# A hybrid attention and state-space layer: half of the opening's adaLN rows as TensorE products, the opening's orders written out, and attention loads one step ahead

## The chip, the cores and the metric

The kernel runs on one core of a Trainium2 chip. Its time is the device time of one execution in microseconds. Three runs of the kernel before were timed; the profile is of one more execution. The engines are TensorE (PE, with its weight loads as PEld), VectorE (DVE), ScalarE (ACT), GpSimd (POOL) and SyncE (SP), which issues nearly all DMA transfers. Each engine works through its own queue in order.

## The reference, cut to what matters

One layer over 2048 tokens of width 1024, in f32, and one conditioning vector `c`:

```python
mod = jax.nn.silu(c) @ w_ada[layer] + b_ada[layer]          # 1024 -> 6 * 1024
shift1, scale1, gate1, shift2, scale2, gate2 = jnp.split(mod, N_MOD, axis=-1)
h = modulate(rmsnorm(x, norm1_w[layer]), shift1, scale1)    # h * (1 + scale) + shift
x = x + gate1[:, None, :] * hybrid_mixer(h, ...)            # q, k, v, z, x/B/C, dt = h @ w_in
h = modulate(rmsnorm(x, norm2_w[layer]), shift2, scale2)    # attention and an SSD scan
x = x + gate2[:, None, :] * swiglu(h, w_gate_up[layer], w_down[layer])
return rmsnorm(x, final_norm_w)
```

`q` and `k` are turned by rotary tables (`rope`) whose angles come from `positions`. Nothing of the mixer can be computed before `shift1` and `scale1`, 2 x 1024 of the 6 x 1024 modulation values, are there.

## The kernel before, in words

The tokens are cut into four blocks of 512 (`b` 0 to 3). Activations stand with the feature on the partition, eight tiles of 128 x 512 per block. Each big product is made from operands split into a high and a low f32r half: `mm3` (L237 to L240) issues three matmuls, high by high, high by low, low by high. `weight` (L222) loads a weight tile into one of 5 `raw` buffers, ACT rounds it into the high half (L230), POOL subtracts for the low half (L231); six `w` buffers hold the pairs. `modulated` (L272) makes one tile of the normalized and modulated input: a DVE product (L274), the high half on ACT (L276), the low half on DVE (L277).

For each block the mixer's projections run one after the other: `queries`, `keys_values`, `convolved`, `gated`. They are Python generators, and PE's order is the order in which the generators are advanced (`manual_schedule` with PE among its engines means that PE issues in program order). `run(main, ratio)` advances a main generator; after each of its steps `tick` advances the side work (attention, the state-space scan, output projection) `ratio` steps, one step of `rest_of_ada`, and counts down the `pending` steps of the next block's norm. Engines that are not under `manual_schedule` get their order from the compiler, which simulates the program and lets a later instruction go ahead when its inputs and buffers are ready.

A modulation value is a dot product of silu(c) with a column of `w_ada`. The transposed matrix lies in memory as 48 rows of 128 x 1024; `ada` (L151) loads one row (512 KB, one DMA) and reduces it on DVE against `csil`, silu(c) copied to all partitions (L154). That gives 128 of the values, one column of `mod`. Columns 8 to 15 are `scale1`, 0 to 7 `shift1`. The other 32 rows are done later by `ada_later` (L156), in two halves of 256 KB with two `aw` buffers (L160, L165).

The opening is `first_norm` (L929) under `manual_schedule` for PE, DVE and SP. Eight tiles of x are loaded; ACT squares each (L940) and PE sums each square over the partitions with 4 products of two columns (L942). `root_of` takes the root on DVE, `spread` (L263) builds a diagonal and copies it over the partitions with one plain f32 product of 512 columns (L269). Then for each of the eight tiles the scale column is finished (L948), the tile modulated, and the reductions of a later pair of rows and the loads of q weights follow. After it `rope_tables` (L177) makes the sine and cosine tables: seven DVE steps each for sine and cosine and one ACT step each (L193), on three `s` buffers.

After the opening `queries(0, h)` (L342) makes q for the four token tiles of block 0 at once, 192 products of 256 columns into all four `d` banks of PSUM, and `rope` (L312) reads each bank with four DVE steps (L321, L322) before it is free. `keys_values` (L367) needs two `d` banks for each half of the block. The loads of x for the next block's norm are held behind the last load of x (`issue_after(last_load.ins)`, L1035).

`attentions` (L466) works through 4 tiles of 128 queries a block. Each starts with the loads of kv and q (L488, L489) and at once transposes both on PE (L493, L501); then come four steps of scores, with the tile before finished in between.

Of the kernel before, what the change touches and what calls it, by code (L numbers as in the profile page):

```python
# [17 lines left out]
P = 128  # L18
S = 2048
D = 1024  # L20
# [22 lines left out]
def hymba_layer(ctx, tc, xT, crow, pos, wada, vecs, rows, wq, wkv, wz, wx, wo, wgu, wd4, wd2, outT):  # L43
# [57 lines left out]
    vec = const([P, 116], "vec", pool=cst)  # L101
# [8 lines left out]
    conv_b, snw = vec[:, 104:112], vec[:, 112:116]  # L110
# [32 lines left out]
    def silu_c(i):  # L143
        cs, th = csil[:, i * T:(i + 1) * T], big("s", 3, pool=fw)
        nc.scalar.activation(th, cs, AF.Tanh, scale=0.5)
        nc.vector.scalar_tensor_tensor(cs, th, 1.0, cs, ALU.add, ALU.mult)
    mod = const([P, 48], "mod", pool=cst)
# [3 lines left out]
    def ada(i, m):  # L151
        w = m().rearrange("p h t -> p (h t)").bitcast(F32)
        nc.sync.dma_start(w, wada[i])
        nc.vector.tensor_tensor_reduce(w, w, csil, 0.5, b_ada[:, i:i + 1], ALU.mult, ALU.add, mod[:, i:i + 1])  # L154

# [21 lines left out]
    def rope_tables():  # L177
        posf = const([P, S // P], "posf", pool=ip)
        nc.vector.tensor_copy(posf, posi)
        ang = big("s", 3, pool=fw)  # L180
# [3 lines left out]
        for dst, turn in ((sin, 0.0), (cos, 0.25)):  # L184
            k, r = big("s", 3, pool=fw), big("s", 3, pool=fw)
# [6 lines left out]
            nc.vector.tensor_scalar(r, r, PI_IN, -PI_IN, ALU.min, ALU.max)  # L192
            nc.scalar.activation(dst.rearrange("p t j -> p (t j)"), r, AF.Sin)  # L193

# [27 lines left out]
    def weight(src, n, key, store):  # L222
# [8 lines left out]
        nc.gpsimd.tensor_tensor(lo, raw[:, :n], hi.bitcast(F32), ALU.subtract)  # L231
# [40 lines left out]
    def modulated(x, bc, scale, shift, into):  # L272
# [4 lines left out]
        nc.vector.scalar_tensor_tensor(lo, h, shift, hi.bitcast(F32), ALU.add, ALU.subtract)  # L277
# [64 lines left out]
    def queries(b, h):  # L342
        if b == 0:
            qb = [dense() for _ in range(NT)]
            for kp in range(KT // 2):
                ws = first_ws[kp] if kp < len(first_ws) else [weight(wq[c][kp], 512, (f"q{c}", kp), False)
                                                              for c in range(2)]
# [115 lines left out]
    def attentions(b, m):  # L463
# [20 lines left out]
        held = None  # L484
        for t in range(NT):
            gt = b * NT + t
            q, kv = m.m2(), m.m1()
            nc.sync.dma_start(kv, kv_d[gt])  # L488
            nc.sync.dma_start(q, q_d[gt])  # L489
# [19 lines left out]
            for j in range(4):  # L509
# [3 lines left out]
                if j == 3:  # L513
                    probabilities(st, sms, slots)
                yield
# [413 lines left out]
    def first_norm():  # L929
        st, h, x0, ws = side_bank(0), [], [], []  # L930
# [4 lines left out]
        for d in range(2):  # L935
            ada(8 + d, common.m4)
            ada(d, extra.m4)
        for d in range(KT):
            sq = tmp()
            nc.scalar.activation(sq, x0[d], AF.Square)  # L940
            for t in range(NT):
                nc.tensor.matmul(st[:, 2 * t:2 * t + 2], sq[:, t * P:(t + 1) * P], ones[:, 0:2],  # L942
                                 start=d == 0 and t == 0, stop=d == KT - 1 and t == NT - 1, skip_group_check=True)
        y = root_of(st, NT)
        bc = spread(y, bc=side_bank(1))
        ada(10, common.m4)
        for d in range(KT):
            nc.vector.scalar_tensor_tensor(scl1[:, d:d + 1], mod[:, 8 + d:9 + d], 1.0, n1w[:, d:d + 1],  # L948
                                           ALU.add, ALU.mult)
            h.append(modulated(x0[d], bc, scl1[:, d:d + 1], sh1[:, d:d + 1], operand()))  # L950
            if d + 2 < KT:
                ada(2 + d, extra.m4)
            if d + 3 < KT:
                ada(11 + d, common.m4)
            if d % 2 == 0 and d < 6:
# [225 lines left out]
```

## Time and profile before

| | us |
|---|---|
| runs timed, median (lowest, highest) | 2439.4 (2439.01, 2440.95) |
| the profiled execution | 2434.49 |
| its span, first to last instruction | 2432.8 |
| mean granted TensorE clock | 0.965 |
| PE / DVE / POOL / ACT busy | 2261.8 / 1461.9 / 1262.3 / 967.3 |
| first q product on PE | 32.42 |
| first product of keys_values on PE | 98.32 |

Times within the profile count from the start of the span. In the groups by line, the columns after the bar are busy time, mean ns of one, and the idle time of the engine just before, with what ended it. In a timeline the columns are start, duration, engine, line, operation, output and inputs; in brackets stands the idle time before it and what ended that. In the list of waits: us in total, how often, and the longest. In the table of windows each engine's busy time in that stretch stands with its number of instructions. PE's matmuls overlap, so their rate is read from one start to the next, not from the duration. A helper's instructions all have the helper's line: L238 to L240 are every split product.

### The profile page before, as it was taken

To read this page: it belongs to the slowest core of one execution; us is meant where nothing else is said; L and a number is where in the kernel's file an instruction comes from. 1 tells how busy PE (TensorE), PEld (TensorE's weight loads), DVE (VectorE), ACT (ScalarE), POOL (GpSimd) and SP (SyncE) were. 2 spreads that over 40 slices of the span, in tenths; PEclk is the share of its full clock that TensorE was granted. 3 is DMA by queue.
4 is the path that set the end of the run, shared out by engine and by line. 5 is a ranking of instruction groups with operands and counts; after the bars stand their busy time and mean duration, and the time that the engine had idled before them with its cause. 6 is when DMAs were issued, how large, how long until landed. Compare 5 with 4: busy or idle time off the path is not lost.

```text
span 2432.8 us, 33013 instructions
## 1 busy us (share of the span) xinstructions
PE 2261.8 (93%) x11254; PEld 1891.9 (78%) x11254; DVE 1461.9 (60%) x2519; ACT 967.3 (40%) x2004; POOL 1262.3 (52%) x1249
## 2 busy tenths in 40 slices
PE   6587999999999799999999999899899999999996
PEld 5567989887988588888887877677688888878785
DVE  7876874764445965578675434438855555554544
ACT  2354552655245545433334323224333333333332
POOL 3653743534122864679885234137766666643432
PEclk9798999999999799999999999999899999999998
DMA  7699866868874322233235555764322222263441
GB/s 274 210 331 316 294 228 204 279 218 275 287 241 159 96 78 83 81 111 100 88 95 167 197 177 158 249 206 136 130 87 84 86 79 78 78 228 98 145 157 53
DMA packets 244457, 403.82 MB, mean 166 GB/s; under 512 B 21952, under 2 KB 68032, under 8 KB 244288
## 3 DMA queue, kind: packets, MB, share of 16 engines
q1 hardware_dynamic: 243136, 400.66, 50.0%
q8 instruction: 89, 1.46, 0.2%
q10 hardware_dynamic: 1152, 1.05, 0.1%
q14 instruction: 80, 0.66, 0.1%
HBM read 307.19 MB, written 94.44 MB: 165 GB/s over the span
## 4 chain that ended last, share of the span: by engine, by line
PE 77%; DVE 8%; DMA 5%; issue 4%; POOL 3%; ACT 3%; SPq 1%; POOLq 0%; DVEq 0%; ACTq 0%
PE d L238 11%; PE d L240 11%; PE d L239 11%; PE d L803 8%; PE d L805 8%; PE d L804 8%; PE am L238 1%; PE am L239 1%; PE am L240 1%; POOL w L231 1%; PE at L574 1%; DMA t<-act 1%; DMA t<-in_xT_dram 1%; PE sm L683 1%; PE st L803 1%
## 5 line engine op out<-in xcount | busy, mean ns | idle before, releaser
L752 ACT ACTIVATE w<-raw 128x512 fp32r<-128x512 f32 x308 | 193.5, 630 | 531.7 <-PE d L240 251.0
L803 PE MATMUL d<-b,w 128*128 128x512 f32 x924 | 372.7, 405 | 17.4 <-ACT b L783 9.6
L804 PE MATMUL d<-b,w 128*128 128x512 f32 x924 | 370.8, 401 | 7.2 <-DVE b L779 5.1
L805 PE MATMUL d<-b,w 128*128 128x512 f32 x924 | 368.9, 399 | 0.0
L238 PE MATMUL d<-a,w 128*128 128x512 f32 (+1 forms) x720 | 281.1, 398 | 12.4 <-ACT a L871 11.5
L239 PE MATMUL d<-a,w 128*128 128x512 f32 (+1 forms) x720 | 281.5, 391 | 1.7 <-DVE a L747 1.7
L240 PE MATMUL d<-a,w 128*128 128x512 f32 (+1 forms) x720 | 282.3, 392 | 0.0
L753 POOL TENSOR_TENSOR w<-raw,w 128x512 fp32r<-128x512 f32 x88 | 120.1, 1365 | 304.8 <-ACT w L752 292.0
L753 POOL TENSOR_TENSOR w<-s,w 128x512 fp32r<-128x512 f32 x132 | 188.6, 1429 | 126.1 <-ACT w L752 117.6
L882 DVE SCALAR_TENSOR_TENSOR x<-d,mod,x 128x512 f32<-128x512 f32 (+1 forms) x182 | 130.9, 725 | 197.6 <-PE d L240 197.3
L238 PE MATMUL d<-w,hl 128*128 128x256 f32 (+1 forms) x640 | 194.8, 304 | 43.3 <-DVE s L322 19.9
L803 PEld LDWEIGHTS d<-b,w 128*128 128x128 f32 x924 | 175.9, 191 | 60.6 <-ACT b L783 13.3
L753 DVE TENSOR_TENSOR w<-raw,w 128x512 fp32r<-128x512 f32 x220 | 191.1, 869 | 43.3 <-ACT w L752 40.7
L804 PEld LDWEIGHTS d<-b,w 128*128 128x128 f32 x924 | 176.4, 191 | 46.7 <-DVE b L779 6.8
L805 PEld LDWEIGHTS d<-b,w 128*128 128x128 f32 x924 | 176.5, 191 | 39.9
L240 PE MATMUL d<-w,hl 128*128 128x256 f32 (+1 forms) x640 | 190.8, 298 | 4.6 <-DVE hl L277 4.6
L239 PE MATMUL d<-w,hl 128*128 128x256 f32 (+1 forms) x640 | 189.7, 296 | 0.0
L238 PEld LDWEIGHTS d<-a,w 128*128 128x128 f32 x720 | 137.1, 191 | 47.5 <-ACT a L871 15.5
L238 PEld LDWEIGHTS d<-w,hl 128*128 128x128 f32 x640 | 130.8, 204 | 48.4 <-issue 20.9
L239 PEld LDWEIGHTS d<-a,w 128*128 128x128 f32 x720 | 136.8, 190 | 34.4 <-DVE a L747 2.8
L248 POOL TENSOR_TENSOR t<-t 128x512 f32<-128x512 f32 (+1 forms) x84 | 106.7, 1271 | 108.5 <-ACT t L247 104.8
L240 PEld LDWEIGHTS d<-a,w 128*128 128x128 f32 x720 | 136.2, 189 | 30.3
(311 smaller groups left out, 5427.7 us busy)
## 6 DMA issues: line engine op xcount, KB each, us to landing
raw<-in_wgu_dram SPq DMA_DIRECT2D x176, 256.0 KB, 2.7
raw<-in_wd_dram SPq DMA_DIRECT2D x176, 256.0 KB, 2.7
w<-w_x SPq DMA_DIRECT2D x48, 512.0 KB, 4.9
w<-w_o SPq DMA_DIRECT2D x48, 512.0 KB, 4.6
act<-t SPq DMA_DIRECT2D x88, 256.0 KB, 2.1
t<-act SPq DMA_DIRECT2D x88, 256.0 KB, 4.7
t<-in_xT_dram SPq DMA_DIRECT2D x80, 256.0 KB, 4.3
aw<-in_wada_dram SPq DMA_DIRECT2D x64, 256.0 KB, 3.8
```

What stands on the lines that cost most here:

```text
L231: nc.gpsimd.tensor_tensor(lo, raw[:, :n], hi.bitcast(F32), ALU.subtract)
L238: nc.tensor.matmul(out, ahi, bhi, start=first, stop=False)
L239: nc.tensor.matmul(out, ahi, blo, start=False, stop=False)
L240: mm3.last = nc.tensor.matmul(out, alo, bhi, start=False, stop=last)
L248: eng.tensor_tensor(acc, acc, sq, ALU.add)
L574: nc.tensor.transpose(ps[:, (2 * s + r) * P:(2 * s + r + 1) * P], sm[:, r, s, :], ident)
L752: nc.scalar.activation(hi, x, AF.Copy)
L753: eng.tensor_tensor(lo, x, hi.bitcast(F32), ALU.subtract)
L803: nc.tensor.matmul(out, ahi, bhi, start=first and k == 0, stop=False, skip_group_check=True)
L804: nc.tensor.matmul(out, ahi, blo, start=False, stop=False, skip_group_check=True)
L805: mm3.last = nc.tensor.matmul(out, alo, bhi, start=False, stop=k == 3, skip_group_check=True)
L882: nc.vector.scalar_tensor_tensor(x, ps, gate2[:, c:c + 1], x, ALU.mult, ALU.add)
```

## The change

- The 16 rows of the first modulation: those of `mod` columns 8 to 13 and 0 to 5 that belong to tiles 2 to 5 stay reductions on DVE (`rows_of`, `reduced`: 8 rows). The other 8 rows (tiles 0, 1 and 6, 7) come as TensorE products: a new input `wadk` holds those columns of `w_ada` untransposed, in two batches of 4 loads of 512 KB. PE multiplies each 128 x 512 half load with one column of silu(c) (`ccol`) into one PSUM line, 8 products a batch; ACT copies the line out, PE turns it into columns by four small products, and three short DVE steps finish `mod` and `scl1`.
- The squares are summed over the eight tiles by DVE adds, so that PE sums over partitions with 4 calls.
- `opening` replaces `first_norm`, with ACT too in program order, and with the q products placed inside: PE's order is 4 sums, 6 products of the first batch, the spread, 2 products, the turning, q products of tiles 0 to 3, the second batch, its turning, q products of tiles 4 to 7.
- The low halves of block 0's q weights are made on DVE, not POOL.
- Half of the rotary tables is made at the very start, the other half after the last modulation; the tables and silu(c) use `m2` buffers, not `s`.
- q of block 0 takes two `d` banks and the side banks `sm` and `st`.
- What follows the opening, up to and with `keys_values(0)`, the start of `rest_of_ada` and the next block's norm, is under `issue_after(first_done.ins)`: its DVE instructions stand behind the last modulation. The norm of block 1 is begun after keys_values, with its later steps at ticks 11 and 15, not 17 and 21.
- `attentions` loads the first kv and q with two empty steps ahead of their use, and those of each later tile in the middle of the tile before.

```diff
+    def ada_loads(batch):
+        ws = [extra.m4().bitcast(F32) for _ in range(KT // 2)]
+        for w, src in zip(ws, wadk[batch]):
+            nc.sync.dma_start(w.rearrange("p h t -> p (h t)"), src)
+        return ws
+
+    def ada_products(ws, out, ks):
+        for k in ks:
+            nc.tensor.matmul(out[0:1, :], ccol[:, k:k + 1], ws[k // 2][:, k % 2, :], start=k == 0, stop=k == KT - 1)
+
+    def ada_columns(out, turned, d):
+        line = tmp()[0:1, :]
+        nc.scalar.copy(line, out[0:1, :])
+        for j in range(4):
+            nc.tensor.matmul(turned[:, 2 * j:2 * j + 2], line[:, j * P:(j + 1) * P], ones[0:1, 0:2], start=True, stop=True)
+        got = turned[:, 0:8].rearrange("p (j k) -> p j k", k=2)[:, :, 0]
+        for at, src in ((8 + d, got[:, 0:2]), (d, got[:, 2:4])):
+            nc.vector.scalar_tensor_tensor(mod[:, at:at + 2], src, 0.5, b_ada[:, at:at + 2], ALU.mult, ALU.add)
+        nc.vector.scalar_tensor_tensor(scl1[:, d:d + 2], mod[:, 8 + d:10 + d], 1.0, n1w[:, d:d + 2], ALU.add, ALU.mult)
...
-        nc.gpsimd.tensor_tensor(lo, raw[:, :n], hi.bitcast(F32), ALU.subtract)
+        (nc.vector if key[0][0] == "q" and not split_d else nc.gpsimd).tensor_tensor(lo, raw[:, :n], hi.bitcast(F32), ALU.subtract)
...
-            qb = [dense() for _ in range(NT)]
+            qb = [dense(), dense(), side_bank(2), side_bank(3)]
...
-        held = None
+        def load(t):
+            q, kv = m.m2(), m.m1()
+            nc.sync.dma_start(kv, kv_d[b * NT + t])
+            nc.sync.dma_start(q, q_d[b * NT + t])
+            return q, kv
+
+        held, nxt = None, load(0)
+        yield
+        yield
         for t in range(NT):
-            gt = b * NT + t
-            q, kv = m.m2(), m.m1()
-            nc.sync.dma_start(kv, kv_d[gt])
-            nc.sync.dma_start(q, q_d[gt])
+            gt, (q, kv) = b * NT + t, nxt
...
+                if j == 2 and t + 1 < NT:
+                    nxt = load(t + 1)
...
-    def first_norm():
...
+    def opening():
+        accs, h, x0 = tmp(), [], []
         for d in range(KT):
             x = extra.m2()
             x0.append(x)
-            last_load = nc.sync.dma_start(x, xT[0, d])
...
+            nc.sync.dma_start(x, xT[0, d])
+        tables = rope_tables()
+        silu_columns()
+        next(tables)
         for d in range(KT):
...
+            square_into(accs, x0[d], d == 0, nc.vector)
+        first = ada_loads(0)
...
+        for i in range(2):
+            silu_c(i)
+        st, line = side_bank(1), side_bank(0)
+        for t in range(NT):
+            nc.tensor.matmul(st[:, 2 * t:2 * t + 2], accs[:, t * P:(t + 1) * P], ones[:, 0:2], start=True, stop=True)
+        ada_products(first, line, range(0, 6))
         y = root_of(st, NT)
         bc = spread(y, bc=side_bank(1))
...
+        ada_products(first, line, range(6, 8))
+        ada_columns(line, side_bank(0), 0)
+        weights(0)
+        rows = [rows_of(2), rows_of(3)]
+        main = queries(0, h)
+        ready(0)
+        ready(1)
+        next(main)
+        weights(1)
+        reduced(2, rows[0])
+        ready(2)
+        rows.append(rows_of(4))
+        reduced(3, rows[1])
+        ready(3)
+        second = ada_loads(1)
+        next(main)
+        line = side_bank(0)
+        ada_products(second, line, range(8))
+        weights(2)
+        rows.append(rows_of(5))
+        reduced(4, rows[2])
+        ready(4)
+        reduced(5, rows[3])
+        ready(5)
+        ada_columns(line, side_bank(0), 6)
+        weights(3)
+        next(main)
+        ready(6)
+        ready(7)
+        next(main)
+        drain(tables)
+        return h, main
...
-        run(queries(0, h), 0)
-        with tc.issue_after(last_load.ins):
-            nxt = norm_ahead(1, (17, 21))
-        rest = rest_of_ada()
-        ada_rest.append(rest)
-        run(keys_values(0, h), 0)
+        with tc.issue_after(first_done.ins):
+            drain(main)
+            rest = rest_of_ada()
+            ada_rest.append(rest)
+            run(keys_values(0, h), 0)
+            nxt = norm_ahead(1, (11, 15))
```

Of the helpers inside `opening` that the cut leaves out, `weights(kp)` fetches and splits two q weight tiles, `rows_of(d)` loads the two rows of tile d into `common` `m4` buffers (there are four), `reduced(d, two)` reduces them and finishes `scl1`, and `ready(d)` is one `modulated`. `first_done` is the last DVE instruction of the last `modulated`.

More of the change, by code (lines that the diff above doesn't have):

```diff
@@ L143, in silu_c, with silu_columns @@
     def silu_c(i):
-        cs, th = csil[:, i * T:(i + 1) * T], big("s", 3, pool=fw)
+        cs, th = csil[:, i * T:(i + 1) * T], common.m2()
         nc.scalar.activation(th, cs, AF.Tanh, scale=0.5)
         nc.vector.scalar_tensor_tensor(cs, th, 1.0, cs, ALU.add, ALU.mult)
+    def silu_columns():
+        th = small([P, KT], "csc", 1, pool=ip)
+        nc.scalar.activation(th, ccol, AF.Tanh, scale=0.5)
+        nc.vector.scalar_tensor_tensor(ccol, th, 1.0, ccol, ALU.add, ALU.mult)
     mod = const([P, 48], "mod", pool=cst)
@@ L183, in rope_tables @@
                                 invf.unsqueeze(1).broadcast_to([P, S // P, HALF]), ALU.mult)
-        for dst, turn in ((sin, 0.0), (cos, 0.25)):
-            k, r = big("s", 3, pool=fw), big("s", 3, pool=fw)
+        turns = []
+        for turn in (0.0, 0.25):
+            k, r = common.m2(), common.m2()
             nc.vector.tensor_scalar(k, ang, 1.0 / (2 * math.pi), turn, ALU.mult, ALU.add)
@@ L276, in modulated @@
         nc.scalar.activation(hi, h, AF.Identity, bias=shift)
-        nc.vector.scalar_tensor_tensor(lo, h, shift, hi.bitcast(F32), ALU.add, ALU.subtract)
+        modulated.last = nc.vector.scalar_tensor_tensor(lo, h, shift, hi.bitcast(F32), ALU.add, ALU.subtract)
         return hi, lo
@@ L343, in queries @@
         if b == 0:
-            qb = [dense() for _ in range(NT)]
+            qb = [dense(), dense(), side_bank(2), side_bank(3)]
             for kp in range(KT // 2):
-                ws = first_ws[kp] if kp < len(first_ws) else [weight(wq[c][kp], 512, (f"q{c}", kp), False)
-                                                              for c in range(2)]
+                ws = first_ws[kp]
                 for e in range(2):
@@ new lines, in opening, with weights, rows_of, reduced @@
+        first = ada_loads(0)
+        def weights(kp):
+            first_ws.append([weight(wq[c][kp], 512, (f"q{c}", kp), False) for c in range(2)])
+        def rows_of(d):
+            m = common.m4().rearrange("p h t -> p (h t)").bitcast(F32)
+            n = common.m4().rearrange("p h t -> p (h t)").bitcast(F32)
+            nc.sync.dma_start(m, wada[8 + d])
+            nc.sync.dma_start(n, wada[d])
+            return m, n
+        def reduced(d, two):
+            for i, w in zip((8 + d, d), two):
+                nc.vector.tensor_tensor_reduce(w, w, csil, 0.5, b_ada[:, i:i + 1], ALU.mult, ALU.add, mod[:, i:i + 1])
+            nc.vector.scalar_tensor_tensor(scl1[:, d:d + 1], mod[:, 8 + d:9 + d], 1.0, n1w[:, d:d + 1],
+                                           ALU.add, ALU.mult)
@@ L947, in first_norm @@
[L947 to L955, printed above, removed]
-                ws.append([weight(wq[c][d // 2], 512, (f"q{c}", d // 2), False) for c in range(2)])
@@ L957, in first_norm @@
-        return h, last_load, ws
-    with tc.manual_schedule(engines={mybir.EngineType.PE, mybir.EngineType.DVE, mybir.EngineType.SP}):
-        for i in range(2):
-            silu_c(i)
-        h, last_load, first_ws = first_norm()
-        rope_tables()
+        ada_products(first, line, range(6, 8))
[7 more added lines that the diff above has]
+        weights(1)
@@ L965, in hymba_layer @@
+        ready(7)
+        next(main)
+        drain(tables)
+        return h, main
+    first_ws = []
+    with tc.manual_schedule(engines={mybir.EngineType.PE, mybir.EngineType.DVE, mybir.EngineType.SP,
+                                     mybir.EngineType.Activation}):
+        h, main = opening()
+        first_done = modulated.last
     nc.scalar.activation(neg_a, a_log, AF.Exp)
@@ L1131, in _layout @@
     out["wada"] = a(w_ada[0].T.reshape(48, P, D))
+    wk = w_ada[0].reshape(D, 6, 4, 2 * P)
+    out["wadk"] = a(np.stack([np.concatenate([wk[:, 1, i], wk[:, 0, i]], axis=1) for i in (0, 3)])
+                    .reshape(2, 4, 2, P, T).transpose(0, 1, 3, 2, 4).reshape(2, 4, P, 2 * T))
     cols = lambda v, n: v.reshape(n, P).T
```

26 lines of the change are left out of this document (11 added, 15 removed).

## The prediction

> **What bounds the kernel now.** I read the page's busy line and strip first, then the windows for the start, then who PE waited for, and last the timelines of the start.
>
> ```profile
> PE 2261.8 (93%) x11254; PEld 1891.9 (78%) x11254; DVE 1461.9 (60%) x2519; ACT 967.3 (40%) x2004; POOL 1262.3 (52%) x1249
> ...
> PE   6587999999999799999999999899899999999996
> ```
>
> PE carries the run: 9 tenths nearly everywhere. The exception is the left end, where the first two slices (61 us each) stand at 6 and 5. The windows there, whose columns are PE, PEld, DVE, ACT, POOL busy, granted clock, DMA share and GB/s:
>
> ```profile
> 0.00:32.40 32.40, 15.86 (x66) 14.23 (x66) 17.73 (x37) 9.36 (x16) 7.54 (x51) 1.00 0.89 343
> 32.40:78.70 46.30, 35.26 (x192) 32.17 (x192) 41.64 (x70) 12.02 (x20) 17.01 (x11) 0.82 0.60 189
> 78.70:98.30 19.60, 0.01 (x1) 0.01 (x1) 18.60 (x31) 6.61 (x10) 10.96 (x8) 0.60 0.62 202
> 98.30:112.40 14.10, 13.76 (x95) 13.49 (x96) 10.53 (x32) 4.75 (x9) 14.10 (x16) 0.83 0.57 186
> 100.00:240.00 140.00, 111.02 (x659) 99.39 (x659) 97.98 (x240) 68.66 (x157) 79.59 (x80) 0.90 0.91 315
> ```
>
> Up to 32.4 DMA works (0.89). From 32.4 to 98.3 DVE does: 60.2 us busy of 65.9, while PE does the 192 q products and then nothing for 19.6 us. Who PE waited for says why:
>
> ```profile
> PE d L238 <- DVE s L322: 19.9, 2, 19.6
> ...
> PE d L238 <- DVE so L411: 8.6, 2, 6.7
> ...
> PE am L493 <- DMA m<-kv: 8.4, 1, 8.4
> ...
> PE at L501 <- DMA m<-q: 2.3, 2, 1.4
> ```
>
> The first line is the gap. The q products fill all four `d` banks; rope must read one before keys_values has a bank; rope needs the tables, which DVE makes only after the last modulation, between rows of `ada_later`. The critical path of the opening is thus DVE: modulations, tables, rope, then PE.
>
> **The opening of the new kernel up to the first q product.**
>
> ```profile
> L940 ACT ACTIVATE t<-m x8: 612/629/630, 8.3 to 12.7; 128x512 f32<-128x512 f32 x8
> ```
> ```profile
> 9.09 13.79 PE L942 MATMUL am<-ones,t 128*128 128x2 f32 x64 [9.09 <-ACT t L940]
> ```
> ```profile
> L942 PEld LDWEIGHTS am<-ones,t x64: 288/333/338, 9.1 to 22.5; 128*128 128x128 f32 x64
> ```
> ```profile
> 754.48 1.02 PE L269 MATMUL sm<-t,ones 128*128 128x512 f32 x2
> 755.34 1.02 PE L269 MATMUL st<-t,ones 128*128 128x512 f32 x2
> ...
> 1638.11 2.05 PE L269 MATMUL am<-t,ones 128*128 128x512 f32 x2
> ```
> ```profile
> 76.65 0.69 DVE L182 TENSOR_TENSOR s<-posf,invf 128x512 f32<-128x512 f32 x1
> ```
> ```profile
> 124.40 0.57 ACT L393 COPY cin<-d 128x512 f32<-128x512 f32 x1
> ```
> ```profile
> 32.42 0.58 PE L238 MATMUL d<-w,hl 128*128 128x256 f32 x1 [2.08 <-ACT hl L276]
> ```
>
> The squares end at 13.3 as before (12.7 plus 0.63); their adding up, now on DVE, trails by one add of 0.69: 14.0. The first half of the tables lies ahead of that, while x still lands, and is covered. The 32 column sums of L942 (13.79 us, 0.43 a call) become four: 15.7.
>
> Next come eight products of a one-column weight with 512 columns of plain f32, with the spread after the sixth. None is in this trace; the nearest is the spread, L269, also plain f32 by 512: 0.86 us from one call to the next in the first two rows, and in the third one call with its tail takes 2.05, twice one row's 1.02, so I put a call there at 1.7. Nine calls cost 7.7 or 15.3. I take the higher price: L942's weight loads, at the same place and of the same type, took 333 ns (median, none under 288) from beginning to end. So 31.0, with 23.4 kept for the range. The root of the mean lies beside the first six.
>
> Then ACT copies the line (0.57), four small products turn it (0.43 each), and three short DVE steps, 0.5 as an estimate from the 0.69 of a wide one, give the modulation: 33.8. ACT is now in program order, so the casts of the first q weights and the first `hi` queue behind that copy. Two `lo` of weights now on DVE (1.4), one product and its `hi` (1.4) bring the first q product to 36.6. It was 32.42: this part loses 4.2.
>
> **From there to the end of the q products.**
>
> ```profile
> 41.12 1.28 DVE L154 CUSTOM_DVE_ANT_0 m<-m,csil,vec 128x1024 f32<-128x1024 f32 x1
> ...
> 47.50 2.31 DVE L154 CUSTOM_DVE_ANT_0 m<-m,csil,vec 128x1024 f32<-128x1024 f32 x1
> ...
> 50.98 0.75 DVE L274 SCALAR_TENSOR_TENSOR t<-m,scl,at 128x512 f32<-128x512 f32 x1
> 52.52 0.75 DVE L277 SCALAR_TENSOR_TENSOR hl<-t,mod,hl 128x512 fp32r<-128x512 f32 x1 [0.79 <-ACT hl L276]
> 53.19 1.28 DVE L154 CUSTOM_DVE_ANT_0 m<-m,csil,vec 128x1024 f32<-128x1024 f32 x1
> ...
> 73.95 1.82 DVE L277 SCALAR_TENSOR_TENSOR hl<-t,mod,hl 128x512 fp32r<-128x512 f32 x1
> ```
> ```profile
> 62.00 0.28 PE L240 MATMUL d<-w,hl 128*128 128x256 f32 x1
> 62.12 0.28 PE L238 MATMUL d<-w,hl 128*128 128x256 f32 x1
> ```
>
> DVE's list is written out by hand: the first `lo` 0.75; `ready(1)`, 2.2 as from 50.98 to 53.19, the wait for ACT inside; six `lo` of q weights, 4.1; four pairs of reductions at 2.6, 10.4; six more `ready`, 13.2; the second columns, 0.5. Together 31.2: 67.8.
>
> ```profile
> 45.16 6.99 POOL L231 TENSOR_TENSOR w<-raw,w 128x512 fp32r<-128x512 f32 x4 [8.65 <-ACT w L230]
> ```
>
> On top I count 4 us because POOL (kv weights, and perhaps the next block's norm, which the hold leaves free on ACT, POOL and SP) slows DVE's two-input steps: the reduction at 41.12, without POOL, took 1.28, the one at 47.50, under this row, 2.31. It is 0 if POOL rests, 12 if a dozen are hit.
>
> And 3 us, between 0 and 6, for the third pair of q weights. SP is in order: `rows_of(4)` waits for a buffer that the first reduction of `reduced(2)` frees, at 42.2 by the list above (36.6 + 0.75 + 2.2 + 1.4 + 1.28). Behind it stand the second batch, `weights(2)`, `rows_of(5)`, `weights(3)` and the kv weights. Its 1 MB, the batch's 2 and the weights' 0.5 take 10.2 at 343 GB/s, to 52.4, and a cast of 0.63 follows: 53.0. DVE is through `ready(3)` at 50.6 and waits 2.4, with both reductions 4 and 5 queued behind.
>
> The last `lo` is then at 74.8 (75.8 before); its 24 products at 0.12 end at 77.6. The second batch of products starts once the fourth column's are done, 53.4, and has until `ready(5)`, some 14 us; all at the higher price, 13.7, it just fits, so it costs nothing on the path.
>
> Now keys_values can start at once: two of its banks are free, since q took `sm` and `st`. Half of the tables is left (at most seven steps of 0.69) and the rope; both lie beside the first half of keys_values. Start 77.6 against 98.3: **20.7 gained**.
>
> **After that.**
>
> ```profile
> 98.32 0.56 PE L238 MATMUL d<-w,hl 128*128 128x264 f32 x1 [19.61 <-DVE s L322]
> ...
> 101.10 0.42 PE L238 MATMUL d<-w,hl 128*128 128x264 f32 x1
> 101.76 0.42 PE L238 MATMUL d<-w,hl 128*128 128x264 f32 x1
> ...
> 103.84 0.28 PE L238 MATMUL d<-w,hl 128*128 128x264 f32 x1
> 104.20 0.28 PE L238 MATMUL d<-w,hl 128*128 128x264 f32 x1
> ```
> ```profile
> L165 DVE CUSTOM_DVE_ANT_0 aw<-aw,csil,vec 128x512 f32<-128x512 f32 x10 | 8.5, 847 | 0.4 <-DMA aw<-in_wada_dram 0.2
> ...
> L165 DVE CUSTOM_DVE_ANT_0 aw<-aw,csil,part 128x512 f32<-128x512 f32 x10 | 7.6, 761 | 1.6 <-DMA aw<-in_wada_dram 1.6
> ```
> ```profile
> L248 POOL TENSOR_TENSOR t<-t 128x512 f32<-128x512 f32 x6 | 8.7, 1444 | 11.8 <-ACT t L247 11.7
> ```
>
> Without the gap PE stays at full speed: seven groups of three products at 0.66 become 0.36, 2.1 gained. The first attention's wait for its keys, 8.4, lies four ticks later in PE's order, two chunks of the convolution; the load can land meanwhile. But this stretch is also full of transfers, so something else may be late there: between 0 and 8.4, I take half, 4.2. Loading one step ahead saves up to 2.3 of q waits: 1. It holds one `m2` buffer more, seven of eight by my count of what lives at that step, so I count no loss; the two empty steps cost nothing, as PE has main products beside them.
>
> ```profile
> t<-in_xT_dram SPq DMA_DIRECT2D x80, 256.0 KB, 4.3
> aw<-in_wada_dram SPq DMA_DIRECT2D x64, 256.0 KB, 3.8
> ```
>
> Against that, what filled the gap moves behind the last modulation: ten rows of `ada_later` (16.1 us of DVE, twenty transfers, 5 MB) and the next block's norm (8.7 us of POOL, eight transfers, 2 MB). DVE's rope, dt and rows queue behind the hold; PE waits for them only through banks. In 100 to 240 PE waited for DVE at L411 and for transfers; 8.6 us of DVE waits over 98 busy is 0.09 a us, 1.4 for these rows; 10.7 of DMA waits over 44 MB is 0.24 a MB, 1.7 for 7 MB; with 1.4 for POOL I count 4.5. Ends: 0 (work that is only added there can't gain), and all 24.8 exposed.
>
> Sum: -20.7 - 2.1 - 4.2 - 1 + 4.5 = **-23.5**. The profiled execution took 2434.5 (span 2432.8); it becomes 2411. It lies 4.9 under the median of the runs, so against 2439.4 I forecast **2416 us**.
>
> **Rivals.**
>
> *PE speeds up within the first batch.* Its products stream 512 columns each, L942's streamed two. After the gap keys_values went from 0.66 to 0.36 within 5.5 us (98.32 to 103.84). If the batch does so, three calls cost 1.7 and six 0.86: 10.3 in place of 15.3, and the time is 2411. Against it: L942 ran 13.79 us without a pause at 333 ns throughout; the clock column, 1.00 up to 32.4, doesn't settle it. The Trainium skill, TensorE: Matmul & The Clock Gate, Part 1, states that the clock doubles after about 3.4 us of sustained activity; by that rule the nine calls would take some 9.4 us and the time would be 2410. The products at 98.32 agree with it, L942's row as it stands does not.
>
> *Given back in the transfers.* If DMA is the bound from 100 to 240 (share 0.91 at 315 GB/s, thus 346 at full share), 7 MB more cost 20 us there in place of the 4.5: -8, 2431. For it: the share. Against it: only 10.7 us of PE's waits name a transfer, and the rows are not urgent and hold two buffers. The same time would come if the hold did not hold and ten rows still ran ahead of the last modulation, 1.6 each.
>
> *DVE takes over: slower.* From 100 to 240 DVE is busy 98 of 140; with 16.1 more, in a stretch some 25 shorter, it would have no slack. If it then sits in its queue's waits as long as now, the 16.1 are exposed; if POOL's 8.7 are too, and half of the twenty moved reductions are slowed by 1 us under them, 10, the sum is -20.7 - 2.1 + 34.8 = +12: 2451. It decides once DVE's share there passes some 0.85. Against it: of PE's waits only 8.6 name L411.
>
> **How the numbers follow.** Forecast 0.45; the faster batch, or the whole 8.4 saved, 0.22; given back 0.22, of which half comes out within 0.2% (4.9 us, about what a measurement of this kernel can tell from no change); DVE 0.11. So faster 0.78, same 0.11, slower 0.11. Low end: the faster batch (2411), the other 4.2 of the key wait and the 4.5 not due give 2402. High end: past the second rival to no change, 2439; the slower case and what lies under 2402 are left out.
>
> **What would show it.** Right: the first q product near 37; the last modulation near 75; no idle over 2 us at the first keys_values product, near 78; no PE wait of 8 us on the first keys; L165 starting only after the last modulation and reaching past 270. Wrong: weight loads of 189 ns within the first batch; L231 on DVE waiting over 6 us for the third q pair; DVE over 0.85 and long PE waits on L411 or L578 before 240; or a span gain far under the gain at keys_values.

## The result, and the profile after

The changed kernel takes 2444.97 us (median of 10 runs, 2442.28 to 2454.61), the kernel before 2439.2 beside it (10 runs). The ratio is 1.0035, with a 95% interval from 1.0025 to 1.0045: slower, by about 8.5 us, where 2416 was forecast. The profiled execution took 2443.26, its span 2441.5 (2432.8 before), its mean granted clock is 0.964. Three single runs of the experiments below, one each of e1, e2 and e4, took 2864 to 10232 us and are left out of the ratios.

The page's line of the engines and its strip, after:

```profile
PE 2268.4 (93%) x11246; PEld 1885.1 (77%) x11246; DVE 1458.9 (60%) x2521; ACT 969.3 (40%) x2007; POOL 1248.2 (51%) x1241
...
PE   5787999989899799999999999899799999999996
```

The second slice (61 to 122 us) went from 5 to 7. But the ninth and the eleventh, 488 to 549 and 610 to 671, went from 9 to 8. The windows, with the columns as in the prediction, say how much:

```profile
78.70:98.30 19.60, 14.79 (x94) 13.37 (x93) 15.55 (x36) 8.45 (x15) 17.16 (x16) 0.87 0.76 229
200.00:220.00 20.00, 7.30 (x34) 6.38 (x33) 7.98 (x23) 8.93 (x28) 2.99 (x3) 0.65 0.60 222
```

The empty 19.6 us are gone: PE works there for 14.79. Further on, from 200 to 220, there is a new hole: PE is busy for 7.30 of 20 us there, where it was for 15.62 before. PE's idle time is the length of a window less its busy time. The same two stretches, first of before, then of after:

```profile
0.00:200.00 200.00, 133.02 (x710) 117.64 (x710) 152.35 (x319) 78.60 (x153) 105.05 (x142) 0.88 0.80 277
200.00:850.00 650.00, 605.51 (x3752) 537.21 (x3753) 408.63 (x958) 319.86 (x782) 277.69 (x388) 0.95 0.71 234
```
```profile
0.00:200.00 200.00, 152.37 (x830) 123.96 (x831) 141.98 (x300) 85.03 (x168) 95.99 (x139) 0.91 0.81 280
200.00:850.00 650.00, 585.36 (x3580) 519.29 (x3580) 413.20 (x972) 312.72 (x763) 270.40 (x379) 0.94 0.71 231
```

Up to 200 us PE idles 47.6 us, not 67.0: 19.4 less. From 200 to 850 it idles 64.6, not 44.5: 20.1 more. The whole span has 2.1 us more of idle time and 6.6 more of PE work, together its 8.7. The work is mostly the opening's own: its new products (L169, L176, L1002) keep PE busy for 20.8 us, the column sums that they replace took 13.8. By one product that both kernels have, the spread ahead of the MLP at 754.48 before and at 755.99 after, the 20.6 us of the first keys_values product are all gone. Who PE waited for, before and then in the changed kernel:

```profile
PE d L238 <- ACT hl L276: 14.8, 8, 2.9
...
PE am L238 <- DVE k_ring L497: 0.7, 1, 0.7
```
```profile
PE d L269 <- ACT hl L307: 18.3, 5, 9.4
...
PE am L269 <- DVE k_ring L532: 11.4, 5, 3.9
...
PE am L528 <- DMA m<-kv: 6.4, 1, 6.4
PE d L269 <- DMA w<-w_kv: 5.9, 1, 5.9
```

Before, `w_kv` was not in the list. In sum the wait for `hl` grew by only 3.5 us, k_ring by 10.7, `w_kv` by 5.9. The longest single one, 9.4, is the hole at 200. It is not all new: the kernel before has its own wait near there, the first row below, which is 1.3 in the changed kernel. ACT and PE there, before (PE) and after (ACT, then PE):

```profile
202.47 0.58 PE L238 MATMUL d<-w,hl 128*128 128x256 f32 x1 [6.69 <-DVE so L411]
```
```profile
201.68 0.51 ACT L599 ACTIVATE m<-m,ast 128x256 f32<-128x256 f32 x1 [2.12 <-DVE ast L595]
...
206.34 3.30 ACT L605 ACTIVATE m<-m,ast 128x256 f32<-128x256 f32 x8 [0.53 <-DVE ast L602]
209.55 0.70 ACT L307 ACTIVATE hl<-t,mod 128x512 fp32r<-128x512 f32 x1
```
```profile
200.65 0.28 PE L271 MATMUL d<-w,hl 128*128 128x256 f32 x1
210.31 0.58 PE L269 MATMUL d<-w,hl 128*128 128x256 f32 x1 [9.37 <-ACT hl L307]
```

`queries(1)` needs the next modulated tile of block 1. ACT makes its high half only after a whole softmax of the attention, 201.68 to 209.6, and PE, in program order, stands still.

### The profile page after: what moved, and what is told of

Same layout as the page of the kernel before. It is cut to its first block, busy times and chain, and to the rows that moved or that the text cites. A ratio compares the mean times of both kernels' runs of the same rounds, so it can differ in the third digit from the quotient of the medians.

```text
span 2441.5 us, 33030 instructions
## 1 busy us (share of the span) xinstructions
PE 2268.4 (93%) x11246; PEld 1885.1 (77%) x11246; DVE 1458.9 (60%) x2521; ACT 969.3 (40%) x2007; POOL 1248.2 (51%) x1241
## 4 chain that ended last, share of the span: by engine, by line
PE 75%; DVE 7%; DMA 4%; issue 2%; POOL 2%; ACT 2%; SPq 0%; DVEq 0%; POOLq 0%; ACTq 0%
PE d L269 10%; PE d L270 10%; PE d L271 10%; PE d L840 8%; PE d L842 8%; PE d L841 8%; PE am L269 2%; PE am L270 1%; PE am L271 1%; DMA aw<-in_wada_dram 1%; DVE b L816 1%; PE sm L720 1%; PE sm L840 1%; PE sm L842 1%; PE sm L841 1%
## 5 line engine op out<-in xcount | busy, mean ns | idle before, releaser
L269 PE MATMUL d<-w,hl 128*128 128x256 f32 (+1 forms) x608 | 182.0, 299 | 27.9 <-ACT hl L307 18.3
L271 PE MATMUL d<-w,hl 128*128 128x256 f32 (+1 forms) x608 | 178.4, 293 | 1.5 <-DVE hl L308 1.5
L270 PE MATMUL d<-w,hl 128*128 128x256 f32 (+1 forms) x608 | 177.9, 293 | 2.0 <-POOL w L262 2.0
L262 POOL TENSOR_TENSOR w<-raw,w 128x512 fp32r<-128x512 f32 (+1 forms) x64 | 87.7, 1376 | 144.6 <-ACT w L261 141.9
```

The source lines that it names most:

```text
L262: (nc.vector if key[0][0] == "q" and not split_d else nc.gpsimd).tensor_tensor(lo, raw[:, :n], hi.bitcast(F32), ALU.subtract)
L269: nc.tensor.matmul(out, ahi, bhi, start=first, stop=False)
L270: nc.tensor.matmul(out, ahi, blo, start=False, stop=False)
L271: mm3.last = nc.tensor.matmul(out, alo, bhi, start=False, stop=last)
```

## The experiments

All ratios are against the kernel before, run on the same chip in the same session, with 95% intervals. e1 to e4 ran on one chip, e5 to e8 on a second, e9 to e12 on a third, e13 to e18 on a fourth; the kernel before took 2434.6 to 2437.7 us on them, and no other kernel was run on two. Most kernels have 10 to 12 runs, e7 has 5, e10 and e12 have 6. "Opening alone" is the new kernel without its change to the attention.

### Which part

**The opening alone** (the loads at their old place, no empty steps), **the attention alone** (on the kernel before), **no empty steps**, and **no hold**:

```diff
 e1_opening_alone, against the changed kernel
-        held, nxt = None, load(0)
-        yield
-        yield
...
+            q, kv = m.m2(), m.m1()
+            nc.sync.dma_start(kv, kv_d[gt])
+            nc.sync.dma_start(q, q_d[gt])
...
-                if j == 2 and t + 1 < NT:
-                    nxt = load(t + 1)
 e2_attention_alone: the same lines the other way, on the kernel before
 e3_no_empty_steps, against the changed kernel
         held, nxt = None, load(0)
-        yield
-        yield
 e4_no_hold, against the changed kernel
-        with tc.issue_after(first_done.ins):
-            drain(main)
+        drain(main)
```

> The changed kernel with the attention loads put back to the head of each tile and without the two empty steps. Theory A (the opening's gain of about 20 us is lost at the first queries of block 1, because the modulated tiles of that block aren't ready that early, and attention has no part in it): still no gain, within 5 us of the changed kernel's 2445, and keys_values of block 0 starting near 78. Theory B (the attention change, by shifting its steps and loads against the main work, takes what the opening gains): 2415 to 2425.

> The kernel before with only the attention loads one step ahead and the two empty steps. Theory A: between 2434 and 2441, the 8.4 us key wait partly saved. Theory B: 2447 to 2465, slower by what it takes from the opening in the changed kernel.

> The changed kernel without the two empty steps, loads still one step ahead. Theory A: 2440 to 2450, as the changed kernel. Theory B in the form that the two steps put the softmax burst of ACT (8.8 us) in front of the modulation of block 1: the wait of 9.4 us at the first queries of block 1 goes, 2430 to 2437; the first keys are waited for again, some 8 us.

> The changed kernel with nothing held behind the last modulation: rows of ada_later may run among the opening's DVE steps again. Theory A: the last modulation comes 5 to 15 us later, but ten rows are done before it, and from block 1 on times differ by less than 5 us from the changed kernel: 2440 to 2450. A third theory, that the moved rows (16 us of DVE, 5 MB) are what costs the time between 200 and 290: 2430 to 2437.

Measured: opening alone 2431.86, ratio 0.9983 [0.9971, 0.9995]; attention alone 2438.62, 1.0017 [1.0003, 1.0031]; no empty steps 2434.8, 0.9994 [0.9982, 1.0007]; no hold 2437.21, 1.0010 [0.9999, 1.0021]. The opening gains, but some 4 us, not 20. So neither theory of e1 came. e2 lies in the range of its theory A, e3 in that of theory B, and e4 between its two. The 1.0017 of e2 and the 0.52% between the changed kernel and e1 say that the attention's part costs. In the opening alone most of the gain ends at one place, the first wait for a K/V tile:

```profile
PE am L523 <- DMA m<-kv: 18.6, 1, 18.6
```

It was 8.4 before. PE is there 16 us earlier (at 102.3, by its transpose at 120.90 less 18.56 of waiting; before at 118.3, 126.74 less 8.45), but the tile is not. At the first keys_values product the opening alone is 21.4 us ahead (76.96 against 98.32), at this transpose 5.8, over the span 2.9. The tile's store and its load, of before and then of the opening alone (issues: first and last start in us):

```profile
L377 SPq DMA_DIRECT2D kv<-so x4: 471/577/988, 114.3 to 126.9; - x4
L488 SPq DMA_DIRECT2D m<-kv x4: 390/768/1332, 120.7 to 136.6; - x4
```
```profile
L407 SPq DMA_DIRECT2D kv<-so x4: 365/904/1072, 107.3 to 116.9; - x4
L518 SPq DMA_DIRECT2D m<-kv x4: 365/686/1384, 115.7 to 123.6; - x4
```

The store came 7.0 us earlier, the load 5.0. What stands ahead of the store is POOL, which adds the two halves of the rotary (L355) between weight splits (L262). From POOL's timeline of the opening alone:

```profile
83.81 1.32 POOL L262 TENSOR_TENSOR w<-raw,w 128x528 fp32r<-128x528 f32 x1 [2.29 <-ACT w L261]
85.08 0.74 POOL L355 TENSOR_TENSOR m<-m,s 128x256 f32<-128x256 f32 x1
85.78 1.30 POOL L262 TENSOR_TENSOR w<-raw,w 128x528 fp32r<-128x528 f32 x1
...
106.13 1.26 POOL L262 TENSOR_TENSOR w<-raw,w 128x512 fp32r<-128x512 f32 x1
107.35 0.32 POOL L355 TENSOR_TENSOR so<-so,s 128x64 f32<-128x64 f32 x1
```

Between these rows none has a wait in brackets. From 78.7 to 98.3 POOL was busy for 10.96 us before and is for 17.16 after: without the gap the splits that PE asks for and the rotary's adds meet on it.

### Is the start of keys_values on the path at all?

Two tests: the rotary adds of block 0 taken off POOL, and PE made late on purpose. The products of the second kind go to a spare bank and are used by nothing.

```diff
 e5_rope_on_vector, against the opening alone
+        eng = nc.vector if gt < NT else nc.gpsimd
         for i, op in ((0, ALU.subtract), (1, ALU.add)):
-            nc.gpsimd.tensor_tensor(d4[:, :, i, :], d4[:, :, i, :], t4[:, :, i, :], op)
+            eng.tensor_tensor(d4[:, :, i, :], d4[:, :, i, :], t4[:, :, i, :], op)
 e7_late_keys, against the opening alone (e10_wait_filled: behind keys_values;
 e12_one_product: range(1); e11_changed_late_keys: on the changed kernel)
             drain(main)
+            spare = side_bank(0)
+            for i in range(10):
+                mm3(spare, h[0][0][:, 0:P], h[0][1][:, 0:P], h[1][0], h[1][1], True, True)
 e9_before_gap_filled: range(14), on the kernel before, ahead of keys_values
```

> The opening alone with the rotary adds of block 0 (8 of q, 8 of k) taken from POOL to DVE. Theory A, the gain is lost on POOL: in the opening alone POOL is busy without a gap from 83.8 to 110 us with weight splits and these adds, the first K/V tile is stored at 107.3 and PE waits 18.6 us for it to come back. Then the store comes at 98 to 101, the wait falls to 9 to 12, and the end comes 5 to 9 us before the opening alone: ratio 0.9945 to 0.997. Theory B, transfers set the pace (their share is 0.95 from 112 to 200 us): the wait turns into others, ratio 0.998 as for the opening alone.

Measured: 2430.32, 0.9979 [0.9970, 0.9988]: the wait for the tile fell to 6.2 us, and the time stayed. The store came at 105.1, two us earlier and not six to nine; the wait turned into another, as theory B had it, but not for its reason: the new one, 11.2 us, is for a bank that DVE's rotary (L356) has not read, not for a transfer.

> The opening alone with 30 products of 512 columns more (about 12 us of TensorE, into a spare bank) between the first q and the K/V products: PE reaches K/V 12 us later and nothing else is moved. Theory A, the gain of the opening runs into the wait for the first K/V tile, which POOL and the way through DRAM set: the wait falls from 18.6 to 6 to 9 us and the time grows by 0 to 4 us, ratio 0.998 to 1.000. Theory B, the gain at K/V carries and is lost elsewhere: the time grows by the 12 us, ratio 1.003.

Measured: 2421.43, 0.9953 [0.9941, 0.9965]. The thirty products are less work than the 12 us that were expected: 0.39 us is the duration of one, but they start every 0.23 us, and all thirty take 6.9 us (79.57 to 86.43). In the same way three take 0.7 us, not 1.2. Neither theory came: with 6.9 us more of work ahead of keys_values the kernel is 7 us faster than without. Theory A was right in that the wait falls (from 18.6 to 6.5) and holds the work. Two reasons were open for the rest: a PE that is kept busy keeps its clock (0.94 from 112 to 200, 0.90 in the opening alone), or the compiler's new order for the other engines. The next four were to part them.

> The kernel before with 42 products of 512 columns more (about 17 us of TensorE into a spare bank) in the gap of 19.6 us ahead of its K/V products, where PE waits for the rotary. Theory A, a PE kept busy keeps its granted clock: the gap holds the work, and what follows runs at a higher clock (0.84 from 100 to 110 us before), so that the time falls by 2 to 6 us, ratio 0.9975 to 0.999. Theory B, the 12 us of the late K/V products helped by the order that the planner then chose: 0.998 to 1.002 here, with no sign foretold.

> The opening alone with the same 30 spare products, now behind the K/V products, in the wait of 18.6 us for the first K/V tile. Theory A, PE kept busy: as with the products ahead of K/V, ratio 0.994 to 0.997, since the wait is filled in either case and only the clock behind it changes. Theory B, the order of the other engines decides: another time, 0.997 to 1.002.

> The changed kernel with the 30 spare products ahead of its K/V products. Theory A, PE kept busy: its wait for K/V is only 6.4 us, so the work fits in part and the time grows by 3 to 8 us, ratio 1.0045 to 1.007. Theory B, the order that the planner chooses decides, and the hole of 9.4 us at 200 us goes or stays with it: anything from 0.996 to 1.006.

> The opening alone with 3 spare products (1.2 us) ahead of K/V: a change with next to no cost of its own that makes the planner set out the other engines' work anew. Theory A, PE kept busy: nothing to see, ratio 0.998 to 0.999 as for the opening alone. Theory B, the planner's order decides: it moves from there by up to 0.3% either way, which would be the noise that any edit of this kernel carries.

Measured: gap filled 2436.34, 1.0003 [0.9992, 1.0015]; wait filled 2423.53, 0.9949 [0.9935, 0.9964]; changed and late 2436.75, 0.9997 [0.9987, 1.0007]; three products 2425.08, 0.9956 [0.9943, 0.9969]. Theory A, that a filled wait keeps the clock, falls by e12: three products (0.7 us) fill no wait (it is still 16.8) and bring as much as thirty do. e10 alone would have agreed with it. e9 does not test it: its 42 products took 9.6 us, PE still waits 12.3 ahead of keys_values, and the first of them again takes 0.56 us, as before. The mean granted clock of the runs does go with their time (0.964 in the kernel before, 0.966 in the opening alone, 0.967 with three products, 0.969 with thirty), though e9 has 0.966 without a gain; whether it is a cause or follows from shorter waits is not shown.

The three and the thirty bear on the first question. The first keys_values product and the first transpose of a K/V tile with thirty products, and with three:

```profile
86.43 0.29 PE L269 MATMUL d<-w,hl 128*128 128x264 f32 x1
...
117.61 0.48 PE L523 MATMUL am<-ident,m 128*128 128x128 f32 x1 [6.52 <-DMA m<-kv]
```
```profile
79.95 0.28 PE L269 MATMUL d<-w,hl 128*128 128x264 f32 x1
...
121.38 0.47 PE L523 MATMUL am<-ident,m 128*128 128x128 f32 x1 [16.76 <-DMA m<-kv]
```

27 products more, 6.2 us of PE's work, put the start back by 6.5 us. The transpose does not come later for it but 3.8 us earlier, and in the opening alone, with the start at 76.96, it stands at 120.90. **The start of keys_values does not set when the first K/V tile is there**: at least 6.5 us of it are slack at this place, so the last part of what the prediction counted there is worth nothing. The times agree with that (0.9953, 0.9956), but their intervals alone would not exclude a cost of up to some 3.6 us.

### The order that an edit happens to get

If 0.7 us of work move the time by 0.27%, then so may any edit. Each family got a second draw with the same three products.

> The kernel before with 3 spare products (1.2 us) in the gap ahead of its K/V products. Theory A, an order drawn anew moves any kernel by up to 0.3%: ratio anywhere from 0.997 to 1.003. Theory B, the three products help only where they follow the new opening (they take a bank that the first attention then waits for, or break up a pile there): 0.999 to 1.001.

> The changed kernel with the 3 spare products. If its 1.0035 is mostly the order it happened to get, 0.998 to 1.001; if the attention's part costs by itself, with its empty steps, 1.002 to 1.004.

> The changed kernel without empty steps, loads ahead kept, with the 3 spare products. If loading ahead costs nothing by itself it comes out as the opening alone with the same products, 0.994 to 0.997; if it costs 0.1 to 0.2%, 0.997 to 0.999.

> The attention's part alone, on the kernel before, with the 3 spare products. If loads ahead with empty steps cost by themselves, 1.001 to 1.003 again; if the 1.0017 of the first try was the order, 0.998 to 1.000.

> The changed kernel with its empty steps in block 0 only and the 3 spare products. If the empty steps cost in blocks 1 to 3, by the waits for k_ring, it comes out as without any empty step, 0.998 to 0.9995; if they cost in block 0, 1.000 to 1.002.

Together, with the empty steps in block 0 only (`if b == 0:` ahead of the two `yield`s; e6, e8 and e17) told below:

| kernel | as it is | three products | thirty products |
|---|---|---|---|
| before | 1 | e13: 0.9994 [0.9979, 1.0009] | |
| attention alone | e2: 1.0017 [1.0003, 1.0031] | e16: 1.0011 [1.0002, 1.0020] | |
| opening alone | e1: 0.9983 [0.9971, 0.9995] | e12: 0.9956 [0.9943, 0.9969] | e7: 0.9953, e10: 0.9949 |
| opening, loads ahead, no empty steps | e3: 0.9994 [0.9982, 1.0007] | e15: 0.9990 [0.9979, 1.0000] | |
| the same, empty steps in block 0 | e6: 1.0017 [1.0005, 1.0028] | e17: 0.9974 [0.9961, 0.9987] | |
| the changed kernel | 1.0035 [1.0025, 1.0045] | e14: 1.0005 [0.9992, 1.0017] | e11: 0.9997 [0.9987, 1.0007] |

Read by rows, the families stay apart: the opening alone lies under before in all four draws (0.9949 to 0.9983), attention alone above it in both, the changed kernel above the opening alone in every pair. Read across, one and the same kernel moves by up to 0.43% for 0.7 us of work. The two sides of such a move ran on different chips, each against the kernel before, so that a part of it may be the chip's. All moves go down or nowhere, so that something in the three products themselves (they take the bank that the first attention needs) may help; that was not tried apart. Of the expectations, e14 came out where its time is mostly the order, e16 where the attention's part costs by itself, e15 where loading ahead costs 0.1 to 0.2%; e17 lies under both of its ranges, and e13 in both. In like draws loading ahead without empty steps costs 0.11 and 0.34% against the opening alone; why is not shown. One such move can be seen. ACT and PE of the changed kernel with three products:

```profile
204.52 0.71 ACT L307 ACTIVATE hl<-t,mod 128x512 fp32r<-128x512 f32 x1
205.15 3.30 ACT L605 ACTIVATE m<-m,ast 128x256 f32<-128x256 f32 x8
```
```profile
205.28 0.58 PE L269 MATMUL d<-w,hl 128*128 128x256 f32 x1 [5.67 <-ACT hl L307]
```

L307 now stands ahead of the eight scalings of L605, not behind them, and PE's wait is 5.67, not 9.37: 3.7 us for one place in a queue, of the 7 that e14 gained.

### Where the attention's part costs

> The changed kernel with its two empty steps in the attention of block 0 only. Theory A, the empty steps cost in the attentions of blocks 1 to 3, by putting each K transpose beside other ACT and DVE work of the mixer (waits for k_ring 11.4 us after, 0.7 before): these waits go to under 5 us and the time comes 8 to 12 us below the changed kernel, ratio 0.9985 to 1.0005. Theory B, they cost in block 0, where they push a softmax ahead of block 1's modulated tile (the wait of 9.4 us at 200 us): it stays at 1.003 to 1.004.

> Both edits on the changed kernel: rotary adds of block 0 on DVE, empty steps in block 0 only. Theory A on both: K/V tile stored at 98 to 101, no wait for it left, waits for k_ring under 5 us, ratio 0.992 to 0.996. If transfers set the pace, or block 1's modulated tile on ACT comes late whatever PE does: 0.998 to 1.002.

Measured: e6 2438.52, 1.0017 [1.0005, 1.0028]; e8 2435.05, 1.0010 [0.9999, 1.0021]; e17 2428.84, 0.9974 [0.9961, 0.9987]. e6 lies between its two theories, e8 in the second of its ranges. e6 kept 8.8 us of k_ring waits, where theory A wanted under 5: with two idle steps in block 0 the attention's steps meet the mixer's at other places from then on. What went in e6 is the wait for `w_kv`. Over all profiles that line is steady: with empty steps in every block (after, e2, e4, e11, e14, e16) PE waits 10.4 to 13.9 us for k_ring and 5.9 to 7.2 for `w_kv`; in block 0 only (e6, e8, e17), 6.4 to 10.2 and 0 to 2.9; with none (eleven kernels, before among them), 0.7 to 4.3 and at most 0.6. This does not hang on the draw. Not every microsecond of it is time lost, though: e17 has 10.2 us of k_ring waits and is faster than e15, which has 4.3. What the kernels with empty steps in every block have over e17 is the wait for `w_kv`. For `w_kv` the place can be read on SP, in the changed kernel and then without empty steps:

```profile
630.73 0.37 SPq L510 DMA_DIRECT2D mix<-m  x1
...
635.75 3.32 SPq L746 DMA_DIRECT2D t<-mix  x7
639.36 0.81 SPq L407 DMA_DIRECT2D kv<-so  x2
640.66 0.32 SPq L257 DMA_DIRECT2D w<-w_kv  x1
```
```profile
619.60 0.37 SPq L510 DMA_DIRECT2D mix<-m  x1
```

The attention of block 1 ends two steps later, its last store is issued at 630.73 and not at 619.60, the output projection's reloads wait for it, and the last K/V weights stand behind them; PE gets them at 646.5, 5.95 us late. By that reading the late end of the attention is what `w_kv` waits for. One more place goes with the empty steps and not with the draw. From the spread ahead of the MLP (754.48 before, 755.99 after) to the first product of its down projection (1332.05, 1339.10) PE takes 583.0 to 584.5 us in the six kernels with empty steps in every block and 576.8 to 578.7 in all fourteen others; of the 5.5 us that lie between the changed kernel and the one before some 2 are idle time, the rest is PE work that has moved into this stretch. The empty steps do hide the K/V wait (15.6 to 18.6 us in e1, e3, e12 and e15 without them; 3.9 to 6.4 in the changed kernel, e4, e6, e14 and e17 with them). In every block they still cost 0.41 and 0.15% in like draws; in block 0 only, 0.23% more in one draw and 0.16% less in the other.

> The opening alone with the rotary adds of block 0 on DVE and the 3 spare products. If the earlier K/V tile carries to the end, 0.992 to 0.994; if what follows takes it back, as in the first try of these adds, 0.995 to 0.998.

Measured: 2429.9, 0.9979 [0.9967, 0.9991], above the 0.9956 that the opening alone reaches with the same products: the adds on DVE are no gain in either draw, as the second expectation had it. PE then waits 12.8 us (to 105.85) ahead of a product of the convolution, for a bank that the rotary (L356) has not read.

**The best version** measured is thus the opening without the attention's part and with a few spare products: 2421 to 2425 us, 0.5% under the kernel before (0.9949 to 0.9956), 0.8% under the changed one.

## Why the prediction was wrong

**The first q product: 36.6 forecast, 32.52 measured.** The price of the plain f32 products was the one of the rival, not mine. PE's timeline after:

```profile
17.66 7.20 PE L169 MATMUL am<-m,vec 128*1 128x512 f32 x12
24.80 1.12 PE L300 MATMUL at<-t,ones 128*128 128x512 f32 x2
25.85 1.88 PE L169 MATMUL am<-m,vec 128*1 128x512 f32 x4
...
32.52 0.58 PE L269 MATMUL d<-w,hl 128*128 128x256 f32 x1 [3.07 <-ACT hl L307]
```

A call has two rows: six took 7.20 and the spread after them 1.12; all nine 10.2, where the rival had 10.3 and I 15.3. The weight loads show where it turned, and by how much: 328 ns in the sums ahead of the batch and 188 in the spread within it, and in the batch itself, which began at 17.66, rows 0.86 us apart up to 21.04 and 0.43 from 21.70 on:

```profile
L1002 PEld LDWEIGHTS at<-ones,t 128*128 128x128 f32 x8 | 1.8, 328 | 15.9 <-issue 15.9
...
L300 PEld LDWEIGHTS at<-t,ones 128*128 128x128 f32 x2 | 0.3, 188 | 0.9 <-issue 0.9
```
```profile
20.18 0.13 PEld L169 LDWEIGHTS am<-m,vec 128*1 128x1 f32 x1 [0.73 <-issue]
21.04 0.13 PEld L169 LDWEIGHTS am<-m,vec 128*1 128x1 f32 x1 [0.73 <-issue]
21.70 0.09 PEld L169 LDWEIGHTS am<-m,vec 128*1 128x1 f32 x1 [0.54 <-issue]
22.13 0.08 PEld L169 LDWEIGHTS am<-m,vec 128*1 128x1 f32 x1 [0.34 <-issue]
```

The Trainium skill, TensorE: Matmul & The Clock Gate, Part 1, says that the clock doubles after some 3.4 us of sustained activity, and this batch agrees: by the rows above it turned 3.4 to 4.0 us after its start. Why L942's two-column products stayed at 333 ns for 13.79 us no run here shows.

**From there to the last `lo`: 74.8 forecast, 71.70 measured** (70.95 and 0.75), 39.2 us after the first q product where I had 38.2. The wait for the third q weights was 5.07, not 3:

```profile
51.33 1.35 DVE L262 TENSOR_TENSOR w<-raw,w 128x512 fp32r<-128x512 f32 x2 [5.07 <-ACT w L261]
...
63.93 0.23 DVE L179 SCALAR_TENSOR_TENSOR mod<-am,vec 128x2 f32<-128x2 f32 x2 [1.64 <-PE am L176]
```

Of the 4 us of collisions with POOL some 1.8 came: under POOL's only row there, 63.64 to 66.75, two `lo` took 2.40 and not 1.28, and a short step (L180) 0.86 and not 0.16; the reductions beside a resting POOL took 1.28. The second batch cost 1.64 on DVE's path where I had nothing.

**The first keys_values product: 77.6 forecast, 77.72 measured, by luck.** The last `lo` came 3.1 us earlier than forecast, and by the forecast's own 2.8 us for the 24 products behind it keys_values would have begun at 74.5. But PE was not through with the tiles before:

```profile
62.03 1.86 PE L176 MATMUL am<-ones,t 1*128 1x2 f32 x8 [5.89 <-ACT t L174]
63.82 0.58 PE L269 MATMUL d<-w,hl 128*128 128x256 f32 x1
```

The copy of the second batch's line (L174) stands in ACT's written order behind the `hi` of tile 5, at 61.41. PE waits 5.89 us for it, and all 96 q products of tiles 4 to 7 stand behind: 13.9 us without a wait, to 77.72. That "it costs nothing on the path" was wrong by the 3.2 us between 74.5 and 77.72. After that three products took 0.37 us, as forecast.

**The step that failed** is "Start 77.6 against 98.3: 20.7 gained" as a term of the whole. It took the end of one wait for the end of the stretch. Behind it stood a second chain, POOL's rotary adds among its splits, the store and the load of the first K/V tile, which came only 5 us earlier: of the 21.4 us in the opening alone 5.8 are left at the transpose that reads this tile, and e7 against e12 shows the last 6.5 us of the start to be worth nothing there. The sum had -18.3 for the opening (-20.7 - 2.1 + 4.5) and -5.2 for the attention's part (-4.2 - 1); measured are -4.1 for the opening alone, -4 to -12 over its four draws, and +12.7 for the attention's part on top of it. The prediction's own sign for this, "a span gain far under the gain at keys_values", came.

**The key wait** ("the load can land meanwhile", 4.2 of 8.4 saved) went the other way without the empty steps, to 18.6; with them it is 6.4, 2.0 saved. **The empty steps at nothing** ("PE has main products beside them") was wrong: PE's products did hide them, but they put the side work two steps later against everything that waits for its end: 6 to 7 us for `w_kv`, some 2 us of idle time beside the MLP, and 10 to 14 us of waits for k_ring, of which it is not shown how much costs time. **The moved rows and norm, 4.5**: no run puts them back alone. The rows ran from 72.0 to 340.0, past 270 as foretold (29.4 to 269.8 before). From 100 to 240 the DMA share was 0.90 (0.91 before), DVE was busy for 96.30 us (97.98), and PE for 108.53 (111.02). So neither "given back in the transfers" as a bound of bandwidth nor "DVE takes over" is what came, though the sign of the latter did: PE's waits for L441, which is L411 before, fell from 8.6 to 1.6. What took the gain back is one wait after another, each on another engine.

**Not settled**: why the opening alone moves between 0.9983 and 0.9949 with a few products, and how much of the changed kernel's 1.0035 is a poor draw: against the opening alone in like draws the attention's part costs 0.44 to 0.52% each time (on the kernel before 0.17% in both draws), but the changed kernel's other two draws came to 1.0005 and 0.9997, not slower than before by what can be measured. That "no hold" came out at 1.0010 lies within such a draw, so that the hold is not judged.

## What to carry to other kernels

A gap on the busiest engine is worth what the second-latest chain at its end leaves of it: before costing a removed wait, follow what the next consumer needs back to its own start (here the tile that goes out to memory and back, and POOL ahead of its store), and test the slack by making the engine late on purpose. Empty steps in a side stream move every later meeting of that stream with the main one, so try them only where the wait is and look at what waits for the stream's end. Where the compiler orders some engines, judge an edit of under half a percent by two or three orders, with a neutral instruction added, before crediting it with the difference.

## What was not expected of the hardware

Plain f32 products of 512 columns sped up from 0.86 us a row to 0.43 some 4 us into their batch, while two-column products ran for 13.79 us in the kernel before without any such change. In the opening alone a K/V tile took 13.6 us from the issue of its store to the transpose that reads it (107.3 to 120.90), 8.4 of them before its load was even issued. And products that nobody uses, 6.9 us of them on an engine that is 93% busy, cost nothing where they stood ahead of a wait.
